# Where in a 128-byte line the matrix operands start: four places for the split weights, and x tiles each 32 bytes further

## The chip, the cores and the metric

The kernel runs on one core of one Trainium2 chip. The metric is the device time of one execution in microseconds, the median of the runs. A second number, the span, is what the hardware profiler shows of one profiled execution, from its first to its last instruction.

The engines are called PE (the matrix engine, with its weight load PEld), DVE (vector), ACT (scalar), POOL (GpSimd) and SP (here the queue that issues most transfers). On-chip memory has 128 partitions; "address" below is the byte address inside a partition, the same for all partitions. "Place" is that address modulo 128, and "line" a stretch of 128 bytes that begins at a multiple of 128.

## What is computed

One encoder layer on x of 256 rows by 2048 columns, all in float32: a half-step SwiGLU feed-forward with layer norm, a mixer (a Hyena group with long convolutions and a differential attention group, both from one input projection, joined by one output projection) with layer norm, and a second half-step feed-forward with layer norm.

```
x = layer_norm(ALPHA * x + 0.5 * swiglu(x, ffn1_w_gate, ffn1_w_up, ffn1_w_down), ln1_g, ln1_b)
proj = x @ w_in
y = concatenate([hyena_group(proj[:, :3072], ...), diff_attention_group(...)], -1) @ w_out
x = layer_norm(ALPHA * x + y, ln2_g, ln2_b)
x = layer_norm(ALPHA * x + 0.5 * swiglu(x, ffn2_w_gate, ffn2_w_up, ffn2_w_down), ln3_g, ln3_b)
...
def swiglu(x, w_gate, w_up, w_down):
    return (silu(x @ w_gate) * (x @ w_up)) @ w_down
```

The feed-forward is 5632 wide, so its six matrices and the two of the mixer are nearly all of the work and of the bytes.

## The kernel before

**Split operands.** PE reads 4-byte operands in a reduced format (F32R). To keep the precision of float32, each operand is held as two tiles: `hi`, the value cast to F32R, and `lo`, what is left of it (`raw - hi`). A product then takes three terms: hi times hi, hi times lo, lo times hi.

**Units.** All weights go through one list of 656 units of 512 KB, in the order of their use. A unit is a tile of 128 partitions by 1024 numbers (4096 bytes in a partition). `nextunit()` hands out the next one; it also lets `fetch` issue the transfers five units ahead (SP queue, four `raw` buffers) and lets `prepare` split two units ahead: ACT casts `raw` into `hi` (L175), DVE subtracts to get `lo` (L176). There are four `hi` and four `lo` buffers (pool `wp`, tags `whi` and `wlo`, four buffers each); a new unit takes whichever buffer was given back first. The framework puts the instructions of each engine into a fixed order when the program is built, and adds the semaphore waits. The last eight units of the program are held at once: four of them use the storage of `xx`, which is free by then.

**Two kinds of product.** In `ws_block` (gate, up and Hyena projections) the weights are the stationary operand and x moves: for each 128-column half `t` of a weight tile, one matmul with `hi` moves the 512 columns of `xx[:, kk]` (256 columns of x hi, then 256 of x lo; L375), and one with `lo` moves the 256 columns of x hi (L376). In `as_block`, in the attention projections and in the output projection, activations are stationary and the weights move, three matmuls of 512 columns each (`mm3`, L94 to L96). In the down projections the stationary tiles are `hh` and `hl`, the split hidden activations.

**Tiles in memory.** `xx` holds the 16 tiles of x transposed, each 2048 bytes in a partition. The helper `line(pool, n)` takes n bytes of filler. With `line(const, 384 - 32 - 192)` behind two small tiles and `line(sm, 384)` in the pool `sm`, every operand of every matmul starts at place 0: `xx`, the four `hi` and `lo` buffers, `hh`, `hl`, `res`, and the tiles of the mixer.

```
i1 = nc.scalar.copy(out=hi[:, s_], in_=raw[:, s_])
i2 = nc.vector.tensor_tensor(out=lo[:, s_], in0=raw[:, s_], in1=hi[:, s_].bitcast(F32), op=ALU.subtract)
```

**Names in the trace.** `hi1g`, `lo1g`, `raw1g` are units of gate and up of the first feed-forward, `hi2g` of the second; `1d` and `2d` of the down projections; `hy`, `at` and `wo` of the Hyena, attention and output projections. `hihy0_1_3` is the Hyena unit of column block 0, part 1, quarter 3. `ps` and `ph` are PSUM tiles of gate/up and Hyena, `pd` of down.

Of the kernel before, what the change touches and what calls it, by code (L numbers as in the profile page):

```python
# [11 lines left out]
F32 = mybir.dt.float32  # L12
F32R = mybir.dt.float32r
# [4 lines left out]
P = 128  # L18
L = 256
D = 2048  # L20
FF = 5632
KD = D // P
# [52 lines left out]
def kernel(ctx: ExitStack, tc: tile.TileContext, a: dict, out: bass.AP):  # L75
    nc = tc.nc

    const = ctx.enter_context(tc.tile_pool(name="const", bufs=1))
    wp = ctx.enter_context(tc.tile_pool(name="wp", bufs=4))
    sm = ctx.enter_context(tc.tile_pool(name="sm", bufs=2))  # L80
# [6 lines left out]
    def line(pool, n):  # L87

        pool.tile([P, n // 4], F32, name="space", tag="space", bufs=1)
# [15 lines left out]
    def after(ins, first):  # L105

        tc.add_manual_dep(ins.ins, first.ins.name, mybir.DependencyInfo(mybir.DependencyClass.NoSync, mybir.DependencyReason.DATA), reason="order")
# [41 lines left out]
    def halves(i, k):  # L149

        return [slice(0, k // 2), slice(k // 2, k)] if i < 2 else [slice(0, k)]
# [10 lines left out]
    def prepare(n):  # L162
        while st["split"] < min(n, len(units)):
            i = st["split"]
            _, k, c, name = units[i]
            late = i - (len(units) - LEAD)
            if 0 <= late < 4:

                hi, lo = (xx[:, 4 * late + 2 * q:4 * late + 2 * q + 2].rearrange("p k a l -> p k (a l)") for q in range(2))
            else:  # L170
                hi = wp.tile([P, k, c], F32R, tag="whi", name=f"hi{name}")
                lo = wp.tile([P, k, c], F32R, tag="wlo", name=f"lo{name}")
            raw = raws.pop(i)
            for s_ in halves(i, k):
                i1 = nc.scalar.copy(out=hi[:, s_], in_=raw[:, s_])  # L175
                i2 = nc.vector.tensor_tensor(out=lo[:, s_], in0=raw[:, s_], in1=hi[:, s_].bitcast(F32), op=ALU.subtract)  # L176
                if hold:
                    after(i1, hold["act"])
                    after(i2, hold["dve"])
            parts[i] = (hi, lo)  # L180
            st["split"] += 1
# [24 lines left out]
    def nextunit():  # L206
        i = st["use"]
        st["use"] += 1
        fetch(i + 1 + AHEAD)
        prepare(i + 1 + READY)  # L210
        tick()
        return parts.pop(i)
# [5 lines left out]

    mhalf = const.tile([P, 2], F32, name="mhalf")
    stats = const.tile([P, 2, 4, 6], F32, name="stats")  # L220
    line(const, 384 - 32 - 192)
    ident = const.tile([P, P], F32, name="ident")
    ones = const.tile([P, P], F32, name="ones")
    pvt = [const.tile([P, P], F32, name="pvt0"), const.tile([P, P], F32, name="pvt1")]


    res = const.tile([P, 2, D], F32, name="res")
    xx = const.tile([P, KD, 2, L], F32R, name="xx")
    xv = a["x"][0].rearrange("(p j) d -> p j d", j=2)
    xt0 = []  # L230
    for kp in range(KD // 2):
# [2 lines left out]
        if kp % 2 == 0:  # L234
            fetch(kp // 2 + 1)

    line(sm, 384)
    make_identity(nc, ident)
    nc.gpsimd.memset(ones, 1.0)
    nc.gpsimd.memset(mhalf, -0.5)  # L240
# [711 lines left out]
    for hf_ in range(2):  # L952
        for s in ("q", "k", "v"):
            ps = [bank(f"pa{hf_}{s}{j}") for j in range(2)]
            for ku in range(KD // 2):
                h, lo = nextunit()
# [22 lines left out]
    for k in range(KD):  # L979
        h, lo = nextunit()  # L980
# [86 lines left out]
```

## Time and profile before

| what | value |
|---|---|
| median of the runs | 1945.64 us (2 runs, 1945.63 and 1945.65) |
| the profiled execution | 1945.09 us |
| its span | 1943.3 us |
| granted TensorE clock, mean | 0.996 |
| DVE, ACT and POOL busy | 63%, 48% and 16% of the span |
| read from HBM | 366.27 MB, 193 GB/s over the span |

The profiled execution's own time is 1.8 us over its span, and 0.55 us under the median. A row of groups reads: line, engine, operation, out<-in, shapes, count, then busy time and the mean of one in ns, then the idle time of the engine ahead of it and what ended it. The duration of a matmul includes its way through the array, so consecutive matmuls overlap: what a matmul costs PE is read from the distance between starts.

### The profile page before, as it was taken

The page shows a single profiled execution, that of the slowest core. Times are in us where ns is not written, and L with a number is a line of the kernel's source. Part 1 is how long each engine was busy: PE and PEld are TensorE (multiplying, and loading weights), DVE is VectorE, ACT ScalarE, POOL GpSimd, SP SyncE. Part 2 cuts the span into 40 slices and gives each one's busy share as a digit, 9 for nine tenths or more (in the row PEclk, how much of TensorE's full clock was granted, in tenths as well). Part 3 has the DMA queues.
Part 4 walks back from the last instruction along what each step waited for, and adds up shares of the span by engine and source line. Part 5 has one row for each costly group of instructions (what it writes and reads, how often), then busy time and mean ns, then how long its engine had stood idle before and what let it go on. Part 6 is the DMA issues. An engine that isn't in the chain of part 4 may idle for free. (4 is left out here: it accounts for less than half of the span.)

```text
span 1943.3 us, 27060 instructions
## 1 busy us (share of the span) xinstructions
PE 1914.9 (99%) x10260; PEld 1644.5 (85%) x10260; DVE 1215.8 (63%) x1538; ACT 927.2 (48%) x1334; POOL 305.3 (16%) x330
## 2 busy tenths in 40 slices
PE   9999999999999999999999999999999999999997
PEld 8888888888888887888888888888888888888885
DVE  5555556555566656889978666755555555544445
ACT  5454444455444445555555544545444454433332
POOL 4212111111100002112222011312111112100001
PEclk9999999999999999999999999999999999999998
DMA  8665656665666656755575445865556565655553
GB/s 285 206 191 188 193 187 198 188 193 185 205 208 226 213 190 203 233 182 157 174 223 166 156 159 158 276 193 187 189 191 194 186 193 185 194 193 193 192 193 118
DMA packets 294699, 376.43 MB, mean 194 GB/s; under 512 B 13264, under 2 KB 222313, under 8 KB 294569
## 3 DMA queue, kind: packets, MB, share of 16 engines
q1 hardware_dynamic: 289832, 361.90, 57.9%
q0 software_dynamic: 4736, 12.82, 2.1%
q8 instruction: 80, 1.31, 0.3%
q14 instruction: 51, 0.41, 0.1%
HBM read 366.27 MB, written 8.39 MB: 193 GB/s over the span
## 5 line engine op out<-in xcount | busy, mean ns | idle before, releaser
L375 PE MATMUL ps<-xx,hi1g 128*128 128x512 f32 x1408 | 490.1, 393 | 2.6 <-ACT hi1g L175 2.6
L375 PE MATMUL ps<-xx,hi2g 128*128 128x512 f32 x1408 | 488.6, 394 | 1.1 <-DVE xx L99 1.1
L376 PE MATMUL ps<-xx,lo1g 128*128 128x256 f32 x1408 | 394.3, 280 | 0.4 <-DVE lo1g L176 0.4
L376 PE MATMUL ps<-xx,lo2g 128*128 128x256 f32 x1408 | 390.0, 277 | 0.0
L176 DVE TENSOR_TENSOR lo2g<-raw2g,hi2g 128x1024 fp32r<-128x1024 f32 x176 | 235.4, 1339 | 179.0 <-ACT hi2g L175 179.0
L176 DVE TENSOR_TENSOR lo1g<-raw1g,hi1g 128x1024 fp32r<-128x1024 f32 (+1 forms) x178 | 232.8, 1309 | 177.6 <-ACT hi1g L175 177.2
L375 PEld LDWEIGHTS ps<-xx,hi2g 128*128 128x128 f32 x1408 | 264.0, 188 | 62.3 <-ACT xt L291 1.3
L375 PEld LDWEIGHTS ps<-xx,hi1g 128*128 128x128 f32 x1408 | 263.8, 188 | 61.5 <-ACT hi1g L175 2.8
L175 ACT CAST hi2g<-raw2g 128x1024 fp32r<-128x1024 f32 x176 | 185.1, 1053 | 187.3 <-PE ps L375 173.6
L175 ACT CAST hi1g<-raw1g 128x1024 fp32r<-128x1024 f32 (+1 forms) x178 | 185.5, 1044 | 178.7 <-PE ps L375 170.5
L376 PEld LDWEIGHTS ps<-xx,lo1g 128*128 128x128 f32 x1408 | 266.8, 190 | 1.2 <-DVE lo1g L176 1.0
L376 PEld LDWEIGHTS ps<-xx,lo2g 128*128 128x128 f32 x1408 | 264.4, 188 | 0.1
L411 POOL TENSOR_TENSOR hf<-hf,sg 128x256 f32<-128x256 f32 x88 | 64.7, 754 | 741.8 <-DVE hf L380 741.7
L176 DVE TENSOR_TENSOR lo2d<-raw2d,hi2d 128x1024 fp32r<-128x1024 f32 x84 | 103.5, 1233 | 111.0 <-ACT hi2d L175 110.9
L175 ACT CAST hi1d<-raw1d 128x1024 fp32r<-128x1024 f32 x88 | 92.7, 1053 | 123.5 <-PE pd L96 114.5
L175 ACT CAST hi2d<-raw2d 128x1024 fp32r<-128x1024 f32 x84 | 88.6, 1055 | 130.6 <-PE pd L96 124.0
L176 DVE TENSOR_TENSOR lo1d<-raw1d,hi1d 128x1024 fp32r<-128x1024 f32 x88 | 107.2, 1222 | 66.0 <-ACT hi1d L175 66.0
L375 PE MATMUL ph<-xx,hihy 128*128 128x512 f32 x384 | 137.5, 401 | 2.1 <-DVE xx L99 1.1
L95 PE MATMUL pd<-lo1d,hh 128*128 128x512 f32 x352 | 137.2, 390 | 0.0
L94 PE MATMUL pd<-hi1d,hh 128*128 128x512 f32 x352 | 137.2, 390 | 0.0
L96 PE MATMUL pd<-hi1d,hl 128*128 128x512 f32 x352 | 137.0, 389 | 0.0
L94 PE MATMUL pd<-hi2d,hh 128*128 128x512 f32 x336 | 130.8, 389 | 0.0
(380 smaller groups left out, 3065.7 us busy)
## 6 DMA issues: line engine op xcount, KB each, us to landing
raw1d<-in_ffn_w_down_dram SPq DMA_DIRECT2D x88, 512.0 KB, 4.3
raw2g<-in_ffn_w_gate_dram SPq DMA_DIRECT2D x88, 512.0 KB, 3.4
raw2g<-in_ffn_w_up_dram SPq DMA_DIRECT2D x88, 512.0 KB, 3.5
raw2d<-in_ffn_w_down_dram SPq DMA_DIRECT2D x88, 512.0 KB, 4.2
raw1g<-in_ffn_w_gate_dram SPq DMA_DIRECT2D x87, 512.0 KB, 3.6
raw1g<-in_ffn_w_up_dram SPq DMA_DIRECT2D x87, 512.0 KB, 4.0
rawhy<-in_w_in_dram SPq DMA_DIRECT2D x48, 512.0 KB, 4.4
rawat<-in_w_in_dram SPq DMA_DIRECT2D x48, 512.0 KB, 4.2
```

Of the source, the lines that this page charges most:

```text
L94: mm(out=o, lhsT=lh, rhs=rh, start=start, stop=False)
L95: mm(out=o, lhsT=lh, rhs=rl, start=False, stop=False)
L96: mm(out=o, lhsT=ll, rhs=rh, start=False, stop=stop)
L175: i1 = nc.scalar.copy(out=hi[:, s_], in_=raw[:, s_])
L176: i2 = nc.vector.tensor_tensor(out=lo[:, s_], in0=raw[:, s_], in1=hi[:, s_].bitcast(F32), op=ALU.subtract)
L375: mm(out=ps[t], lhsT=h[:, k, ts_], rhs=xx[:, kk].rearrange("p a l -> p (a l)"), start=kk == 0, stop=False)
L376: mm(out=ps[t][:, :L], lhsT=lo[:, k, ts_], rhs=xx[:, kk, 0, :], start=False, stop=kk == KD - 1)
L411: nc.gpsimd.tensor_tensor(out=hf, in0=hf, in1=sg, op=ALU.mult)
```

## The change

The `hi` and `lo` buffers get a tag for each place in the rotation of four, with one buffer for each tag: unit i uses the buffers `whi{i % 4}` and `wlo{i % 4}` and no others. Ahead of the tiles of units 1, 2 and 3 a filler of 32 bytes is allocated, so the four pairs of buffers start at places 0, 32, 64 and 96; `hi` and `lo` of one unit have the same place. Each tile of `xx` is 32 bytes longer, so tile kk starts at place 32 * (kk % 4).

```diff
-                hi = wp.tile([P, k, c], F32R, tag="whi", name=f"hi{name}")
-                lo = wp.tile([P, k, c], F32R, tag="wlo", name=f"lo{name}")
+
+                if 0 < i < 4:
+                    wp.tile([P, 8], F32, tag=f"space{i}", name=f"space{i}", bufs=1)
+                hi = wp.tile([P, k, c], F32R, tag=f"whi{i % 4}", name=f"hi{name}", bufs=1)
+                lo = wp.tile([P, k, c], F32R, tag=f"wlo{i % 4}", name=f"lo{name}", bufs=1)
...
-    line(const, 384 - 32 - 192)
+    line(const, 384 - 32 - 192 - 128)
...
-    xx = const.tile([P, KD, 2, L], F32R, name="xx")
+
+    xx = const.tile([P, KD, 2 * L + 8], F32R, name="xx")[:, :, :2 * L].rearrange("p k (a l) -> p k a l", a=2)
...
-    line(sm, 384)
```

Two fillers are cut to make room: 128 bytes of the one in `const`, which keeps `res`, `xx` tile 0 and the `raw` buffers at place 0, and the 384 bytes in `sm`. With the three fillers of 32 bytes, everything behind the weight buffers now starts at place 96: the working tiles of 2048 and 1024 bytes, `hh` and `hl`, and the large tiles of the mixer. No instruction is added or removed.

The built programs hold the same instructions in the same order on PE and POOL, and the same transfers in the same order on SP. On ACT and DVE two neighbouring splits change their order, once in the program, in the first part of the Hyena projection. ACT there, before (`hihy` are casts of units, `pc` sums of a finished product, `fw_hi` a table):

```order
L175 CAST hihy0_1_2_0_6909<-rawhy0_1_2_0_6771 128x1024
L175 CAST hihy0_1_3_0_6944<-rawhy0_1_3_0_6816 128x1024
L379 COPY pc0_6918<-ph0_0_0_6724 128x256
L175 CAST hihy0_2_0_0_6974<-rawhy0_2_0_0_6870 128x1024
L379 COPY pc1_6948<-ph0_0_1_6725 128x256
L102 CAST fw_hi_6720<-c_fwd_raw_6913 128x512
```

and after:

```order
L178 CAST hihy0_1_2_0_6911<-rawhy0_1_2_0_6773 128x1024
L178 CAST hihy0_2_0_0_6976<-rawhy0_2_0_0_6872 128x1024
L382 COPY pc0_6920<-ph0_0_0_6726 128x256
L178 CAST hihy0_1_3_0_6946<-rawhy0_1_3_0_6818 128x1024
L382 COPY pc1_6950<-ph0_0_1_6727 128x256
L102 CAST fw_hi_6722<-c_fwd_raw_6915 128x512
```

The casts of unit `hy0_1_3` and of the unit after it, `hy0_2_0`, have changed places. DVE at the same point, before (`lohy` are the subtractions, `z` the short convolution):

```order
L176 TENSOR_TENSOR lohy0_1_2_0_6910<-rawhy0_1_2_0_6771,hihy0_1_2_0_6909 128x1024
L176 TENSOR_TENSOR lohy0_1_3_0_6945<-rawhy0_1_3_0_6816,hihy0_1_3_0_6944 128x1024
L380 TENSOR_TENSOR pc0_6918<-ph0_0_0_6724,pc0_6918 128x256
L176 TENSOR_TENSOR lohy0_2_0_0_6975<-rawhy0_2_0_0_6870,hihy0_2_0_0_6974 128x1024
L678 SCALAR_TENSOR_TENSOR z0_0_6917<-pc0_6918,pvt0_74,z0_0_6917 128x128 x2
```

and after:

```order
L179 TENSOR_TENSOR lohy0_1_2_0_6912<-rawhy0_1_2_0_6773,hihy0_1_2_0_6911 128x1024
L179 TENSOR_TENSOR lohy0_2_0_0_6977<-rawhy0_2_0_0_6872,hihy0_2_0_0_6976 128x1024
L383 TENSOR_TENSOR pc0_6920<-ph0_0_0_6726,pc0_6920 128x256
L179 TENSOR_TENSOR lohy0_1_3_0_6947<-rawhy0_1_3_0_6818,hihy0_1_3_0_6946 128x1024
L681 SCALAR_TENSOR_TENSOR z0_0_6919<-pc0_6920,pvt0_74,z0_0_6919 128x128 x2
```

The same two units have changed places here. PE used unit `hy0_1_0` ahead of `hy0_0_3` in this part, before and after; so the buffer of `hy0_1_0`, which was handed to `hy0_1_3` before, now belongs to `hy0_2_0`, and `hy0_1_3` has to wait for the buffer of `hy0_0_3`, which PE leaves one unit later.

## Prediction

> **What bounds the kernel now.** I read the page's shares first, then its groups, then the busy time by stage, the waits, and the timeline of PE in single stages.
>
> ```profile
> PE 1914.9 (99%) x10260; PEld 1644.5 (85%) x10260; DVE 1215.8 (63%) x1538; ACT 927.2 (48%) x1334; POOL 305.3 (16%) x330
> L375 PE MATMUL ps<-xx,hi1g 128*128 128x512 f32 x1408 | 490.1, 393 | 2.6 <-ACT hi1g L175 2.6
> L376 PE MATMUL ps<-xx,lo1g 128*128 128x256 f32 x1408 | 394.3, 280 | 0.4 <-DVE lo1g L176 0.4
> L94 PE MATMUL pd<-hi1d,hh 128*128 128x512 f32 x352 | 137.2, 390 | 0.0
> ```
>
> PE is busy for 99% of the span, and the three large groups waited 3.0 us in all. The whole unbusy time of PE is 1943.3 - 1914.9 = 28.4 us. So the time is the number of matmuls times their distance, and a change of addresses can move the total only through that distance, or by making ACT, DVE or a transfer so late that PE waits.
>
> ```profile
> ACT hi1g L175 <- PE ps L375: 170.5, 118, 2.5
> DVE lo1g L176 <- ACT hi1g L175: 177.2, 162, 4.2
> ```
>
> These rows of the waits say who waits in the main stage: ACT waits for PE to give a buffer back, and DVE waits for ACT. PE leads; the splitting has time to spare.
>
> The distance is read from stages without interruption. The columns are us, PE busy (matmuls), clock, DMA share, GB/s; the first window is gate and up of the second feed-forward, the second its down projection.
>
> ```profile
> 1230.00:1680.00 450.00, 450.00 (x2598) 1.00 0.62 195
> 1700.00:1900.00 200.00, 200.00 (x884) 1.00 0.59 195
> ```
>
> In the first, 2598 matmuls are 1299 pairs of 512 and 256 columns: 450 / 1299 = 346.4 ns a pair. In the second a matmul of 512 columns takes 200 / 884 = 226.2 ns. I take a matmul to cost c for each column and s for itself. Then 768c + 2s = 346.4 and 512c + s = 226.2, so s = 2 * (346.4 - 1.5 * 226.2) = 14.2 ns and c = (226.2 - 14.2) / 512 = 0.414 ns. A third place tests this, matmuls of 256 columns in the mixer:
>
> ```profile
> 955.44 0.29 PE L94 MATMUL py<-rha,iv 128*128 128x256 f32 x1
> ...
> 956.03 0.28 PE L96 MATMUL py<-iha,iv 128*128 128x256 f32 x1
> ```
>
> Five steps in 0.59 us are 118 ns each, against 256 * 0.414 + 14.2 = 120. The model holds to 2 ns. What the change can touch is therefore c, s, or an extra piece for a stream that starts off a line.
>
> How much work is touched follows from the code. Gate, up and Hyena are 1408 + 1408 + 384 = 3200 pairs, with x moving. Down (2112), attention projections (576) and output projection (384) are 3072 matmuls with weights moving. Together they have 9472 moving streams. x tiles and weights each stand at place 0 in one case of four, so three quarters, 7104 moving streams, start off a line after the change. The moving and the stationary operand of a matmul are at different places in three quarters of the cases too, also in the down projection, where `hh` is at 96 and the weights go through all four places.
>
> **The change part by part.**
>
> *Two splits in another order.* Timeline of ACT, DVE, SP and PE at that place, each row with start and length in us, and the time to landing of the Hyena units:
>
> ```profile
> 779.12 1.05 ACT L175 CAST hihy<-rawhy 128x1024 fp32r<-128x1024 f32 x1 [1.01 <-PE ph L375]
> 781.66 0.37 ACT L379 COPY pc<-ph 128x256 f32<-128x256 f32 x1 [1.49 <-PE ph L376]
> 781.93 1.05 ACT L175 CAST hihy<-rawhy 128x1024 fp32r<-128x1024 f32 x1
> 783.02 1.23 DVE L176 TENSOR_TENSOR lohy<-rawhy,hihy 128x1024 fp32r<-128x1024 f32 x1 [0.52 <-ACT hihy L175]
> 773.56 0.37 SPq L159 DMA_DIRECT2D rawhy<-in_w_in_dram  x1
> DMA to landing us min/median/max: 3.4/4.4/9.5
> 781.82 0.39 PE L375 MATMUL ph<-xx,hihy 128*128 128x512 f32 x1
> 784.59 0.39 PE L375 MATMUL ph<-xx,hihy 128*128 128x512 f32 x1
> 787.36 0.39 PE L375 MATMUL ph<-xx,hihy 128*128 128x512 f32 x1
> ```
>
> Units on PE are 2.77 us apart, and the three PE rows are the starts of `hy0_1_1`, `hy0_1_2` and `hy0_1_3`. Before, `hy0_1_3` was cast at 779.12. Now it takes the slot of `hy0_2_0`, cast at 781.93 and subtracted at 783.02 to 784.25, and PE wants it at 787.36: 3.1 us to spare. Ahead of it stands the cast of `hy0_2_0`, whose transfer was issued at 773.56 and lands at the latest 9.5 us later, at 783.06. With that worst landing the chain is cast to 784.11, cast of `hy0_1_3` to 785.16, subtraction to 786.4; still 1 us early. Queued behind on ACT is the copy of `pc`, which waits for nothing on PE's path; on SP the transfer into the `raw` buffer of `hy0_1_3` comes free up to 3 us later, for a unit some five units ahead. Cost 0; with the cover gone it would be one unit, 2.8 us.
>
> *A fixed buffer for each unit.* Elsewhere units are used in the order of the list, so the buffer given back first is the one the rotation names. Cost 0.
>
> *DVE, ACT and POOL at shifted places.* In the main stage they have room (above). In the Hyena stage DVE has none. Columns: PE, PEld, DVE, ACT, POOL.
>
> ```profile
> 800.00:930.00 130.00, 126.98 (x765) 112.18 (x764) 121.85 (x222) 68.20 (x110) 23.20 (x19) 0.99 0.57 176
> L877 DVE TENSOR_TENSOR tr0k<-qk0k,rope 128x64 f32<-128x64 f32 x2 | 0.4, 216 | 0.0
> L878 DVE TENSOR_TENSOR tr0k<-qk0k,rope 128x64 f32<-128x64 f32 x2 | 0.4, 217 | 0.0
> L678 DVE SCALAR_TENSOR_TENSOR z<-pc,pvt,z 128x128 f32<-128x128 f32 x48 | 18.0, 414 | 4.8 <-ACT z L671 4.8
> L678 DVE SCALAR_TENSOR_TENSOR z<-pc,pvt,z 128x127 f32<-128x127 f32 x48 | 14.4, 339 | 0.0
> ```
>
> DVE is 94% busy there. But the trace has DVE operands off a line already: L877 reads at 32 bytes and writes at 0, L878 the reverse, and they take 216 and 217 ns; the 127-column form of L678 starts 4 bytes in, and is not slower than the aligned one (339 against 414). From 0 to 0.5% of 122 us, 0.6 us; I take 0.
>
> *Transfers into place 96.* `raw` stays at 0, and only the working tiles move. The nearest row is the start, where ACT waits for x:
>
> ```profile
> ACT xx L278 <- DMA xt<-in_x_t_dram: 5.1, 4, 2.2
> ```
>
> If those landings took twice the wait, 5.1 us more; a gain of as much is the other bound. I take 0, since the rest of the working tiles are loaded yields ahead of their use.
>
> *PE's reads.* No matmul of the trace reads off place 0, so the price is bounded from afar. Above: each stream off a line costs one line more, 32 columns * 0.414 = 13.2 ns, 7104 * 13.2 = 94 us. Below: all of s is a collision of the two reads at the same place, and goes where the places differ, 7104 * 14.2 = 101 us. I take 0, by the nearest rows: DVE's three forms above read and write off a line at no price.
>
> The sum against the profiled execution's own 1945.09 us is 1945.1 us; the median of the runs is 0.55 above it, so 1946.
>
> Here the Trainium skill can be weighed. The trace gives 226.2 ns for 512 columns, of which 14.2 are not columns. "TensorE: Matmul & The Clock Gate", section Back-to-back issue gap, gives N/2.4 + 2.5 ns, 216 ns for 512; the trace is 10 ns above that. By the page "SBUF — State Buffer", section Who interferes with whom, PE has two read ports, for the moving operand and for the weight load, that do not wait for each other. By that rule the rest is no collision and the change gains nothing: 1946, where the lower bound above gives 1845. It speaks against any gain from this change; no run here shows it yet.
>
> **The rivals.**
>
> *A line more for each stream off a line (slower).* Place: the moving reads of `xx`, L375 and L376, and of `hi` and `lo` in L94 to L96. Price: 94 us, 2039 us; if only the cut-off part of the first line counts, the mean of 0, 8, 16 and 24 columns over 9472 streams, 12 * 0.414 * 9472 = 47 us, 1993 us. It decides (2%, 39 us) from 39 / 7104 = 5.5 ns a stream. For it: all PE operands stood at place 0, so nothing in the trace contradicts it. Against it: DVE shows no such price.
>
> *Two reads at one place collide, and the change parts them (faster).* All operands stand at place 0, and s is paid by every matmul whatever its length, as a collision at each weight load would be. Removed in three cases of four it gives 1845 us; half removed 1895. It decides from the same 5.5 ns, 39% of s. Against it: s is the same 14 ns in three stages with different neighbours, as a fixed cost of changing the weights would be; and a stream of 512 columns passes all places of a line 16 times whatever its start.
>
> *ACT or DVE slower in the Hyena stage.* If shifted operands cost DVE 5%, 6 us of the 122 come out on PE: 1952 us. The three DVE forms speak against it.
>
> **How the numbers follow.** No effect on PE's reads: 0.60, with 1940 to 1953 us as its own range (the 5.1 us of the start, and the 6 us of DVE). The slower rival: 0.22, of which 0.04 under 2%. The faster one: 0.15, of which 0.03 under 2%. DVE: 0.03. A measurement of this kernel can tell about 2% from no change; so slower 0.18, faster 0.12, within 2% 0.70. The range should leave out 0.2: faster results over 2% spread from 1845 to 1907, slower ones from 1984 to 2039. From 1885 to 2005 it leaves out 40/62 * 0.12 = 0.08 below and 34/55 * 0.18 = 0.11 above.
>
> **What would show it.** No effect: the windows of the two stages hold 2598 and 884 matmuls to within 1%, and the mean of L375 stays at 393 ns. A line more: the means of L375 and L376 both rise by about 10 ns in gate and up, and L94 to L96 likewise, with single steps that differ with k. A collision removed: 512-column steps fall towards 212 ns. The order: no PE wait at 787. I am wrong if PE's distance moves by over 1% in either direction, or if idle time of PE over 28.4 us grows.

## The result, and the profile after

The changed kernel takes 1969.34 us (two runs, 1968.53 and 1970.15), the kernel before 1945.64 us: ratio 1.0122, 95% interval 1.0078 to 1.0165. It is 1.2% slower, too little for a verdict at 2% and more than the interval leaves to chance. The profiled execution took 1970.15 us with a span of 1968.4 us, 25.1 us over the span before.

The page of the changed kernel, busy time of each engine, and its groups of gate and up, down and the splits (the lines of the code have moved by three):

```profile
PE 1940.0 (99%) x10260; PEld 1651.4 (84%) x10260; DVE 1214.4 (62%) x1538; ACT 925.3 (47%) x1334; POOL 306.2 (16%) x330
```

```profile
L378 PE MATMUL ps<-xx,hi1g 128*128 128x512 f32 x1408 | 494.4, 395 | 2.8 <-ACT hi1g L178 2.8
...
L379 PE MATMUL ps<-xx,lo1g 128*128 128x256 f32 x1408 | 394.9, 281 | 0.0
...
L179 DVE TENSOR_TENSOR lo2g<-raw2g,hi2g 128x1024 fp32r<-128x1024 f32 x176 | 234.5, 1333 | 183.1 <-ACT hi2g L178 183.1
...
L95 PE MATMUL pd<-lo1d,hh 128*128 128x512 f32 x352 | 139.0, 395 | 0.0
```

PE is busy for 25.1 us more (1940.0 against 1914.9), and its unbusy time is 1968.4 - 1940.0 = 28.4 us, as before. The whole loss is therefore in matmuls that follow each other without a gap, at a larger distance. DVE's and ACT's totals are a little smaller than before, so the shifted places cost them nothing. The windows say where the distance grew; first two of the kernel before, beside the one with 2598 in the prediction, then the changed one (us, PE busy and matmuls, clock, DMA share, GB/s):

```profile
60.00:460.00 400.00, 400.00 (x2301) 1.00 0.61 191
...
1720.00:1910.00 190.00, 190.00 (x840) 1.00 0.60 197
```

```profile
60.00:460.00 400.00, 400.00 (x2281) 1.00 0.60 190
1230.00:1680.00 450.00, 450.00 (x2575) 1.00 0.62 198
1720.00:1910.00 190.00, 190.00 (x818) 1.00 0.57 188
```

In gate and up of the second feed-forward a pair of matmuls rises from 346.4 to 450 / 1287.5 = 349.5 ns, and in down a matmul of 512 columns from 226.2 to 190 / 818 = 232.3 ns. From the starts of all matmuls in the trace, with the few gaps left out, the means over the whole program go from 347.4 to 349.8 ns for a pair and from 226.9 to 232.6 ns for a down matmul. Added up over all distances of the two traces, gaps included, the down matmuls take 12.2 us more, the attention and output projections 3.7, the pairs 8.5 and all other matmuls 0.8: 25.2 us, all of it. Six tenths come from the matmuls in which the weights move, most of them in down, where x has no part. Of the 8.5 us, 3.7 lie in the first feed-forward, whose pairs also differ between executions with all operands at equal places (last section), so that part is less certain than the rest.

### The profile page after: what moved, and what is told of

The parts are those of the page before. It is cut to its first block, busy times and chain, and to the rows that moved or that the text cites. A ratio compares the mean times of both kernels' runs of the same rounds, so it can differ in the third digit from the quotient of the medians.

```text
span 1968.4 us, 27060 instructions
## 1 busy us (share of the span) xinstructions
PE 1940.0 (99%) x10260; PEld 1651.4 (84%) x10260; DVE 1214.4 (62%) x1538; ACT 925.3 (47%) x1334; POOL 306.2 (16%) x330
## 5 line engine op out<-in xcount | busy, mean ns | idle before, releaser
L379 PE MATMUL ps<-xx,lo2g 128*128 128x256 f32 x1408 | 394.7, 280 | 0.0
L179 DVE TENSOR_TENSOR lo2g<-raw2g,hi2g 128x1024 fp32r<-128x1024 f32 x176 | 234.5, 1333 | 183.1 <-ACT hi2g L178 183.1
L95 PE MATMUL pd<-lo2d,hh 128*128 128x512 f32 x336 | 132.7, 395 | 0.0
```

The costliest lines, as they stand in the source:

```text
L95: mm(out=o, lhsT=lh, rhs=rl, start=False, stop=False)
L379: mm(out=ps[t][:, :L], lhsT=lo[:, k, ts_], rhs=xx[:, kk, 0, :], start=False, stop=kk == KD - 1)
```

## The experiments

In the expectations, a theory R says that the difference between the start addresses of a matmul's moving and stationary operands counts, a theory A that each address counts by itself, since a start off a line cuts lines. The number behind the letter is the modulus: R256 says that the difference counts modulo 256 bytes. The means in ns of experiments 7, 9 and 11 that have no working beside them are of distances between starts, without the first few matmuls of a group.

**1. The rotation alone.** Fixed buffers in turn, no fillers; everything stays at place 0.

```diff
-                hi = wp.tile([P, k, c], F32R, tag="whi", name=f"hi{name}")
+                hi = wp.tile([P, k, c], F32R, tag=f"whi{i % 4}", name=f"hi{name}", bufs=1)
...
```

> Fixed buffers for each unit (tags by i % 4) and the swapped pair of splits, but every operand at place 0 as before. Both theories of places: no change, 1945 to 1947 us, 226 ns for a down matmul and 346 ns for a pair in gate and up. Rival, that the fixed buffers or the swap cost the time: 1960 to 1970 us with PE idle time over 28 us.

1945.36 us, ratio 0.9987 (0.9976 to 0.9998). The rotation and the two exchanged splits cost nothing: the loss is in the addresses.

**2 to 4. One part of the addresses at a time.** Only x turned. The 16 tiles of x grow by 512 bytes together, so the weight buffers stay at 0 modulo 512; what stands behind them, `hh` and `hl` among it, goes to 384 modulo 512:

```diff
-    xx = const.tile([P, KD, 2, L], F32R, name="xx")
+    xx = const.tile([P, KD, 2 * L + 8], F32R, name="xx")[:, :, :2 * L].rearrange("p k (a l) -> p k a l", a=2)
...
-    line(sm, 384)
+    line(sm, 384 - 128)
```

> Only the tiles of x stand 32 bytes further each; weights and hidden activations stay at place 0. After the whole change a pair in gate and up takes 349.5 ns (346.4 before) and a down matmul 232.3 ns (226.2). Theory A, each stream pays for its own start off a line, the moving one above all: the 3.1 ns of the pair come back whole, +10 us, 1956 us; down stays at 226. Theory R, only the difference of the two places counts: the same four differences occur here, also +10 us. Theory W, only the weights' places count: 1946 us.

Only the weights in four places (fixed buffers as in 1), with what stands behind them at 128 modulo 512:

```diff
+                if i < 4 and (0, 32, 32, 32)[i]:
+                    wp.tile([P, (0, 32, 32, 32)[i] // 4], F32, tag=f"space{i}", name=f"space{i}", bufs=1)
...
+                if i == 3:
+                    wp.tile([P, 32 // 4], F32, tag="space", name="space", bufs=1)
```

> Only the weight buffers stand at places 0, 32, 64 and 96; x and the hidden activations stay at place 0. Theory A (the moving stream pays for its own start): gate and up unchanged at 346 ns, since weights are stationary there; down 231 to 233 ns as after the change, +16 to +20 us, about 1964 us. Theory R (the difference counts): gate and up 349.5 ns and down 232 ns, +28 us, about 1973 us.

Only what stands behind the weight buffers, `hh` and `hl` among it, at 96:

```diff
+                if i == 0:
+                    wp.tile([P, 96 // 4], F32, tag="space", name="space", bufs=1)
```

> Only what lies behind the weight buffers moves to place 96: hidden activations, mixer tiles, working tiles. x and weights at place 0. Theory A for moving streams alone: 1946 us, down at 226 ns. Theory A for stationary reads too, or theory R: down at 233 ns (in the changed kernel moving 0 with stationary 96 took 233 ns), +13 to +15 us, about 1960 us; gate and up unchanged.

They took 1966.65 us (ratio 1.0102, 1.0064 to 1.0139), 1974.56 us (1.0142, 1.0105 to 1.0179) and 1968.42 us (1.0111, 1.0067 to 1.0155). Against the runs of the kernel before on the same chip each part alone costs 20 to 28 us, and all of them together cost 24: a price for each shifted operand would add up. The same windows, for x alone, weights alone and what stands behind:

```profile
1230.00:1680.00 450.00, 450.00 (x2580) 1.00 0.64 197
1720.00:1910.00 190.00, 190.00 (x820) 1.00 0.63 189
```

```profile
1230.00:1680.00 450.00, 450.00 (x2563) 1.00 0.64 197
1720.00:1910.00 190.00, 190.00 (x815) 1.00 0.62 188
```

```profile
1230.00:1680.00 450.00, 450.00 (x2598) 1.00 0.65 199
1720.00:1910.00 190.00, 190.00 (x812) 1.00 0.62 187
```

The third is the clean one: gate and up hold 2598 as before, since x and weights were not touched, and down falls from 840 to 812. The first was a miss of mine. Down should have stayed at 840, because `hi` and `hh` both stand at place 0 of a 128-byte line there; it fell to 820. The only operands moved in down were `hh` and `hl`, by 384 bytes. So 128 bytes is not the period. The third took 8 us more than the 1960 expected: a down matmul rose to 234.3 ns, not 233, and gate and up of the first feed-forward, whose operands all stayed in place, held 2274 matmuls in the first window where the kernel before held 2301; experiment 1 has the same 2274 with no address changed.

**5 and 6. Everything shifted alike.** The filler ahead of all matrix operands is 128, then 32 bytes longer:

```diff
-    line(const, 384 - 32 - 192)
+    line(const, 384 - 32 - 192 + 32)
```

> Every operand 128 bytes further, so all at 128 modulo 512 and all differences 0. Theory R512: 1946 us, 226 ns a down matmul, 346 ns a pair. Theory A512: each operand off 512 bytes, down at 232 to 234 ns, about 1970 us.

> Every operand 32 bytes further, all at 32 modulo 128 and modulo 512, all differences 0. Theory R512: 1946 us. Theory A512: about 1970 us. Rival, lines of 128 bytes count when they are cut: 1970 us here but 1946 us for the kernel shifted by 128.

1945.33 us (ratio 1.0003, 0.9981 to 1.0025) and 1950.28 us (1.0002, 0.9983 to 1.0021), against 15 runs of the kernel before on the same chip, which lay between 1943.5 and 1952.9 us. The windows with every operand off its line by 32 bytes:

```profile
1230.00:1680.00 450.00, 450.00 (x2598) 1.00 0.64 197
1720.00:1910.00 190.00, 190.00 (x840) 1.00 0.64 197
```

Both stages stand as before. In these two shifts the address by itself costs nothing, and theory A falls; what counts is how the two operands stand to each other.

**7. Matmuls alone.** One group of 64 matmuls of 512 columns for each pair of places (then the same with pairs of 512 and 256 columns, groups q):

```python
PLACES = (0, 32, 64, 96, 128, 192, 256, 384)
NAMES = "abcdefgh"
...
for n in range(64):
    mo = pm // 4 + 512 * (n // 2 % 4)
    so = pst // 4 + 128 * (n % 4)
    nc.tensor.matmul(out=ps, lhsT=w[:, so:so + P], rhs=m[:, mo:mo + 512], start=n == 0, stop=n == 63)
```

> Matmuls alone, the layer is left out: 64 groups of 64 matmuls of 512 columns, then 64 groups of 32 pairs (512 and 256 columns), for eight places of the moving operand and eight of the stationary one, 0 to 384 bytes into 512. A place is now counted modulo 512, since e2 moved the hidden activations from 0 to 384 modulo 512, which is still place 0 of a 128-byte line, and the down matmul rose from 226 to 232 ns. Theory A512, each operand pays for a start off 512 bytes: 226 ns only for (0, 0), more in the whole rows and columns. Theory R512, the difference counts: 226 ns on the diagonal, 230 to 235 ns off it. Theory N, addresses cost nothing without ACT, DVE and transfers beside it: 226 ns in all 64 groups.

It took 1682.77 us. The timeline of PE, with the moving operand at 128 (first letter e) and the stationary one at 64, 96, 128, 192, 256 and 384 (second letter c, d, e, f, g, h); start and length in us:

```profile
518.05 14.83 PE L42 MATMUL pec<-m,w 128*128 128x512 f32 x64
532.72 15.09 PE L42 MATMUL ped<-m,w 128*128 128x512 f32 x64
547.65 14.67 PE L42 MATMUL pee<-m,w 128*128 128x512 f32 x64
562.15 15.09 PE L42 MATMUL pef<-m,w 128*128 128x512 f32 x64
577.09 15.04 PE L42 MATMUL peg<-m,w 128*128 128x512 f32 x64
591.96 14.68 PE L42 MATMUL peh<-m,w 128*128 128x512 f32 x64
```

A group lasts from its start to the next one's: `pee`, both at 128, (562.15 - 547.65) / 64 = 226.6 ns a matmul; `pef`, 64 bytes apart, 233.4; `peg`, 128 apart, 232.3. And `peh`, 256 apart, lasts no longer than `pee`. No other engine works in this stretch and the kernel transfers nothing (three packets of instruction code, 0.05 MB, are all that moves), so this is PE with its own two reads. The table sets the map against down in the layer, where the order of the units says which buffer a matmul reads; both columns are distances between starts in the traces, ordered by the address of the stationary operand minus that of the moving one, modulo 256:

| apart, bytes | matmuls alone, ns | down in the layer, ns (kernel) |
|---|---|---|
| 0 | 226.7 | 226.9 (before) |
| 32 | 233.4 | 232.8 (weights alone) |
| 64 | 233.4 | 233.1 (weights alone) |
| 96 | 234.3 | 234.3 (behind alone) |
| 128 | 232.2 to 233.4 | 232.5 (x alone), 233.2 (changed) |
| 160 | 233.3 | 234.2 (changed) |
| 192 | 228.9 | 230.0 (changed) |
| 224 | 233.4 | 233.1 (changed) |

The changed kernel has none of its down matmuls at 0: modulo 256 its four weight buffers stand 128, 160, 192 and 224 bytes from `hh`, a quarter of the work each.

**8. The period tested in the layer.** As in 4, but what stands behind is 256 bytes further:

```diff
+                if i == 0:
+                    wp.tile([P, 256 // 4], F32, tag="space", name="space", bufs=1)
```

> x and the weights at 0, everything behind the weight buffers (hh, hl, q, k, yh and the rest) 256 bytes further instead of 96. The map of matmuls alone gives 226.7 ns for a 512-column matmul whose two operands start 256 bytes apart, as for 0, and 232 to 234 for 32, 64, 96 and 128. Theory R256 (the difference of the two starts counts modulo 256): down stays at 226 ns and the time at before's 1945, within 4 us. Rival R512 (modulo 512): down rises to 231 ns or more and the time to 1960 or more, as with 96 (1968).

1945.98 us (ratio 0.9995, 0.998 to 1.001), where 96 bytes had cost 22:

```profile
1720.00:1910.00 190.00, 190.00 (x840) 1.00 0.63 195
```

Down stays at 840. With the map, in which places 256 bytes apart gave the same step within 1 ns, the period is 256 bytes for matmuls of 512 columns.

**9. Pairs alone.** The form of gate and up, with `hi` and `lo` in eight places each against x at 0:

```python
nc.tensor.matmul(out=ps[t], lhsT=w[:, ho:ho + P], rhs=m[:, mo:mo + 512], start=n == 0, stop=False)
nc.tensor.matmul(out=ps[t][:, :L], lhsT=v[:, lo:lo + P], rhs=m[:, mo:mo + L], start=False, stop=n == 31)
```

> The layer is left out; only pairs of matmuls remain in the form of FFN1's gate and up: 512 columns of x against 128 of hi, then its first 256 against 128 of lo, two PSUM tiles in turn, 64 pairs for each of 64 combinations of the place of hi and of lo (0, 32, 64, 96, 128, 160, 192, 224 bytes past a multiple of 512; x stays at 0). Theory R256: each pair's step is fixed by the two differences, and both at 0 gives before's 346 to 347 ns; the combinations spread over some 340 to 358 ns, those with both at 64 near 343.5, as in the changed kernel. Rival, that the differences of a pair come from what runs beside it (DVE, ACT, DMA): all 64 agree within 2 ns.

It took 1449.48 us. The pairs spread from 344.4 ns (`hi` at 224, `lo` at 0) to 353.4 ns, so the rival is out. But both at 64 took 353.3 ns, where 343.5 was expected, and both at 0 took 353.4 ns, where 346 to 347 was. The groups q of experiment 7 give a hint why: with both weights at one place, 11 of the 12 groups at equal places modulo 256 settled at 353.3 ns and one at 346.7, and at 192 six settled at 348.9 and three at 353.3. A difference allows more than one steady step, so it does not fix the step of a pair.

**10. The best relation tried.** x stays at 0, weights and all behind them 192 bytes further, a difference at which pairs had taken 344.8 ns in the kernel with x alone turned, and in the changed kernel 343.6 ns at one combination of places, though 346.8 to 352.1 ns at the others with the same difference:

```diff
+                if i == 0:
+                    wp.tile([P, 192 // 4], F32, tag="space", name="space", bufs=1)
                 hi = wp.tile([P, k, c], F32R, tag="whi", name=f"hi{name}")
```

> x stays at 0, the weights and everything behind them stand 192 bytes further: the weights are 192 from x in gate, up and Hyena (3200 pairs), hh is 0 from the weights in down, and in the attention projections (576 matmuls) x as the stationary operand is 64 from the weights. Theory R256: a pair at difference 192 from x at 0 took 344 to 345 ns in two earlier kernels, against 347 at difference 0, so -2.5 * 3200 = -8 us; the 576 rise by 6.5 ns, +4 us; down stays at 226 to 227 ns. Time 1941 us, 1936 to 1944, under the kernel before. Rival, that any two starts apart cost as in the changed kernel: gate and up rise to 350 ns a pair, time 1955 or more.

1965.17 us (ratio 1.0095, 1.0078 to 1.0112): slower, where I expected a gain.

```profile
1230.00:1680.00 450.00, 450.00 (x2549) 1.00 0.63 195
1720.00:1910.00 190.00, 190.00 (x840) 1.00 0.62 193
```

Down stays at 840, as the table says for weights and `hh` moved together. Gate and up went to 450 / 1274.5 = 353.1 ns a pair. So 344 ns is not a price of 192 as such: modulo 256 the 343.6 ns of the changed kernel belonged to these very places, weights at 192 and x at 0. What differs is that there x's place changes from tile to tile and the weights' place from unit to unit. Whether the neighbouring matmuls' places count, or the stream settled into the longer of the two steps that the map shows at 192 (348.9 and 353.3 ns), these runs do not separate.

**11. Finer places, and places in alternation.** The moving operand at 0 and the stationary one at 32 places (groups f), then one operand alternating between two places (groups s and m):

```python
def group(name, moving, stationary):
    ...
    for n in range(64):
        mo = moving[n % 2] // 4 + 512 * (n // 2 % 4)
        so = stationary[n % 2] // 4 + 128 * (n % 4)
        nc.tensor.matmul(out=ps, lhsT=w[:, so:so + P], rhs=m[:, mo:mo + 512], start=n == 0, stop=n == 63)
```

> The layer is left out; only matmuls of 512 columns remain, 64 for each group. Groups faa to fdh: moving operand at 0, stationary operand at 0, 4, 8, 16, 24, 32, 48, 64, 80, 96, 112, 128, 144, 160, 176, 184, 192, 200, 208, 224, 240, 248, 252, 256, 288, 320, 448, 512, 704, 768, 1024 and 1280. Groups sa to se: the stationary operand alternates between two places, 0 and 96, 0 and 128, 0 and 192, 96 and 192, 0 and 256; groups ma to me: the moving operand does. Theory R256: 226.7 ns at 0, 256, 512, 768, 1024 and 1280, near 229 at 192, 448 and 704, 232 to 235 elsewhere. Within it, theory N: what collides is the running stream and the load of the next weights beside it, so in sa to sd the stream whose next weights are away from it is the long one. Rival O: a matmul's own two operands decide, so the stream whose own weights are away is the long one. Either way the mean of se and me is 226.7, and that of sa about the middle of 226.7 and 234.3.

It took 649.6 us. Groups of 64, count, busy time in us and mean of one in ns; stationary operand at 248, at 4, and at 256, 0, 240 and 252 bytes:

```profile
L40 PE MATMUL fcf<-m,w 128*128 128x512 f32 x64 | 15.1, 396 | 0.0
...
L40 PE MATMUL fab<-m,w 128*128 128x512 f32 x64 | 15.0, 394 | 0.0
...
L40 PE MATMUL fch<-m,w 128*128 128x512 f32 x64 | 14.7, 389 | 0.0
...
L40 PE MATMUL faa<-m,w 128*128 128x512 f32 x64 | 14.7, 389 | 0.0
L40 PE MATMUL fce<-m,w 128*128 128x512 f32 x64 | 14.7, 389 | 0.0
...
L40 PE MATMUL fcg<-m,w 128*128 128x512 f32 x64 | 14.7, 389 | 0.0
```

The busy time less the last matmul's own length, over 63, is the step: (14.7 - 0.389) / 63 = 227 ns against (15.1 - 0.396) / 63 = 233. All multiples of 256 up to 1280 gave 226.7; four bytes were enough to lose it (232.4). The steps of one group are not equal. Distances of starts in ns, in order:

```
0:    227 227 226 227 227 226
64:   230 236 231 236 231 236
128:  238 229 237 230 237 229
192:  229 232 226 229 232 226
```

They repeat every two to four matmuls. Of the two theories on which read is in the way neither holds: with the stationary operand alternating between 0 and 96 the two steps are 229.0 and 231.0 ns, both long, and with the moving operand alternating between 0 and 192 the mean is 236.7, above each of the single relations (226.7, and 233.4 for 64). So the operands of one matmul alone do not fix its step; the matmuls around it count.

**12. Part of the change with down spared.** x turned as in 2, but what stands behind the weight buffers is at 256, so `hh` is 256 from the weights:

```diff
...
-    line(sm, 384)
+    line(sm, 384 - 256)
```

> As the kernel with the tiles of x alone turned (1966.65 us), but what stands behind x 256 bytes past a multiple of 512 instead of 384, so that hh is 256 from the weights in down, not 384. Theory R256: down (2112 matmuls) and output projection (384) go back from 232.5 to 226.9 ns, 2496 * 5.6 = 14 us, and what is left is x against the weights: 1.8 ns for each of 3200 pairs and the attention projections. Time 1952.7, 1949 to 1957. Rival, that the places of x alone carry the whole loss, through what runs beside them: 1963 to 1968.

1953.95 us, ratio 1.0033 (1.002 to 1.0045), 12.7 us under experiment 2 and inside the 1949 to 1957 expected.

```profile
1230.00:1680.00 450.00, 450.00 (x2580) 1.00 0.63 195
1720.00:1910.00 190.00, 190.00 (x840) 1.00 0.64 195
```

The pairs stand exactly as in 2 (2580), and down is back at 840. The two terms of the loss can be had one without the other. No version here beats the kernel before by more than its own runs differ; the rotation alone, 0.9987 with an interval that ends at 0.9998, comes closest. With all operands at multiples of 256 the kernel before already has the shortest step of a 512-column matmul that the maps show.

## Why the prediction was right, and where it was not

The time fell into the range and the forecast of no change to within 2% held, but the likeliest case (1946 us, own range 1940 to 1953) was not what happened. That the time lies inside 1885 to 2005 is owed to the width that the two rivals gave the range, and is luck as far as the mechanism goes. By the prediction's own sign (PE's distance moves by over 1%) it was wrong: a matmul of down came to cost 2.7% more.

- *What bounds the kernel:* right. The unbusy time of PE is 28.4 us before and after, and the 25 us came through the distance of matmuls, the one way that was left open.
- *Two splits exchanged, fixed buffers:* right, by experiment 1.
- *DVE, ACT and POOL at shifted places:* right. `lo2g` takes 1333 ns, 1339 before. The window of the Hyena stage has DVE as busy as before (121.85 us); columns PE, PEld, DVE, ACT, POOL:

```profile
800.00:930.00 130.00, 126.49 (x761) 112.15 (x760) 121.86 (x226) 70.42 (x113) 18.09 (x13) 0.99 0.57 182
```

- *Transfers into place 96:* right. ACT's wait for x at the start was 5.1 us, and is 5.3:

```profile
ACT xx L281 <- DMA xt<-in_x_t_dram: 5.3, 3, 3.2
```

- *PE's reads:* this step failed. It was taken as 0, between -101 and +94 us, "by the nearest rows: DVE's three forms above read and write off a line at no price". The term measures +25 us. DVE's rows could not carry it: the price is not in reading off a line (experiment 6: everything off by 32 bytes costs nothing) but in where two reads of PE stand to each other, and those rows have no second read of that kind.
- *The count of work touched:* the wrong unit. I counted places modulo 128 and had three quarters of the matmuls at different places. Modulo 256 none of the down matmuls is left at 0, and `hh` at 0 of a line can still be apart (experiment 2).
- *The slower rival*, a line more for each stream off a line, had the sign but not the mechanism: it asked 13.2 ns for each of 7104 streams, and a down matmul rose by 5.7 ns, a pair by 2.4, while a shift of all operands alike cost nothing. The 25 us are short of the 39 us from which it was to decide.
- *The faster rival* had the right thing in view, a meeting of the two reads, with its sign reversed: equal places are the shortest relation for 512 columns, not the collision. No place in the maps brought the mean step of 512 columns under 226.6 ns, so the runs show nothing of the 14 ns that I called s going away; they do not say what it is.

The rule from the Trainium skill, "SBUF — State Buffer", section Who interferes with whom, that PE's port for the moving operand and its port for the weight load are independent, was set against any gain, and none came. As a reason for no effect it does not carry: 226.7 ns turn into 234.3 by moving one operand 96 bytes, with no other engine at work, and the measurement decides.

What stays open: by which part of the memory or of PE the two reads meet, why 240 and 252 bytes are as good as 0 and 248 is not, and what picks the step of a pair. The runs show the relation and its period, not the circuit.

## What to carry to other kernels

In streams of 512-column matmuls keep the start addresses of the moving and stationary tiles at the same value modulo 256: here nearly every other relation cost 2 to 8 ns of 227, and a filler that moved all operands alike cost nothing. For pairs of 512 and 256 columns no such rule follows: alone, equal places mostly took 353.3 ns and 96 bytes apart 346.7, and in the layer equal places mostly took 346.7. When a layout changes, look at every operand that a filler pushes along, since `hh` and what stands with it cost some 20 us alone (experiment 4), and x alone some 7 (experiment 12). And price a read from a row with the same two readers, or time a stream of such matmuls alone; one engine's indifference to a place says nothing about another's.

## What was not expected of the hardware

- The step of a 512-column matmul has a period of 256 bytes in the difference of its operands' addresses; four bytes of it cost 5.7 ns.
- Pairs of 512 and 256 columns with all operands at equal places have two steady steps, 346.7 and 353.3 ns, with little between. Alone they mostly took the longer; the second feed-forward of the kernel before takes 346.7 nearly throughout. In the first feed-forward the profiled executions differ: in that of experiment 1 (1952.04 us) some 850 of the 1408 pairs took 353.3 ns before the stream went over to 346.7, in that of the kernel before (1945.09 us) only a few dozen. One program also differs from execution to execution: runs of the kernel before lay between 1943.5 and 1954.1 us, and the one profiled in experiment 1 lost its time in gate and up of the first feed-forward alone, 400 / 1137 = 351.8 ns a pair against 347.7 in the first window above:

```profile
60.00:460.00 400.00, 400.00 (x2274) 1.00 0.62 189
1230.00:1680.00 450.00, 450.00 (x2598) 1.00 0.65 198
1720.00:1910.00 190.00, 190.00 (x840) 1.00 0.64 195
```
